# A batched 64x64 matmul: the last 768 matrices of a loaded in tiles of 256, all cast on the way

## The chip, the cores and the metric

The kernel runs on one core of one Trainium2 chip. The core has five engines that run their own instruction streams: TensorE (PE in the profile, with its weight loads as PEld), VectorE (DVE), ScalarE (ACT), GpSimd (POOL) and SyncE (SP). Sixteen DMA engines move data between HBM and the on-chip memory SBUF; SP, ACT and GpSimd each issue transfers on a queue of their own (q1, q10 and q0 in the profile), and all three queues run on the same sixteen engines. Matmul results land in PSUM and are copied out by ACT or DVE. The metric is the device time of the run in microseconds.

## The reference

```python
def setup_inputs():
    return {
        "a": np.random.randn(1024, 64, 64).astype(np.float32),
        "b": np.random.randn(1024, 64, 64).astype(np.float32),
    }

def reference(a: np.ndarray, b: np.ndarray) -> np.ndarray:
    return np.matmul(a, b).astype(np.float32)
```

There are 1024 independent products of two 64x64 matrices. Each operand and the result hold 16.8 MB in float32, so 33.55 MB are read and 16.78 MB written.

## The kernel before, in words

The work goes in 16 steps, t = 0 to 15, of 64 matrices each. One step reads 1 MB of b and writes 1 MB of the result; a is loaded for two steps at a time, in tiles s = 0 to 7 of 128 matrices (2 MB of float32). All instructions stand in an order written out by hand (the block from line 210), and each engine runs its own in that order, so an instruction that waits holds up everything behind it on the same engine.

For one step the chain is this. `load_a` brings a tile of a: three quarters (h = 0 to 2) are transfers that GpSimd issues and that turn float32 into bf16 on the way (line 73), the fourth quarter comes as float32 on SP's queue (line 77). A partition reads 16 rows of a matrix in one run: 4 KB of float32. `regroup` (DVE, lines 108 and 111) copies the four quarters into one bf16 tile, `a_bf`, casting the fourth. `transpose(s, j)` lets TensorE transpose pairs of bf16 values as one 32-bit element (line 120, eight transposes for each j), and ACT copies the results from PSUM to `at_sb` (line 123, four copies for a tile). `spread(t)` (DVE, four copies at line 133) places one step's columns of `at_sb` on the diagonal blocks of one of two tiles `at_bd`. `cast(t)` (DVE, line 144) turns b's tile into bf16. `multiply(t)` runs 64 matmuls of 128x128 by 128x64 (line 189) into two PSUM tiles, one for each half step, and evacuates them to `o_sb` (line 177): eight copies on ACT in an even step; in an odd step six on ACT and two on DVE. `store(t)` sends `o_sb` out, one step later, on GpSimd's queue (line 166; the last two steps go on SP and ACT).

b's tiles come on SP for even t and on ACT for odd t (line 96), three steps ahead: `load_b(t + 3)` is issued once `cast(t)` has freed the buffer. The tiles have 3 buffers for a, 3 for b, 2 for `at_sb`, and 8 for `o_sb`, of which the first two hold the first tile of a before the results need them.

Around one even step t = 2s the order is: `spread(t+1)`, `cast(t+1)`, the second half of the transposes of tile s+1, `multiply(t)`, `regroup(s+2)`; in the odd step after it `spread`, `cast`, `multiply`, and the first half of the transposes of tile s+2. So the transposes that stand ahead of a `multiply` on TensorE work on a tile that was regrouped two steps earlier:

```python
            if half == 0 and 0 < s < n_s - 1:
                transpose(s + 1, 1)
            multiply(t)
```

Of the kernel before, what the change touches and what calls it, by code (L numbers as in the profile page):

```python
# [8 lines left out]
fp32 = mybir.dt.float32  # L9
bf16 = mybir.dt.bfloat16  # L10
# [3 lines left out]
def kernel(  # L14
# [14 lines left out]
    nc = tc.nc  # L29
    B, M, K = a.shape  # L30
    _, _, N = b.shape
    assert (M, K, N) == (64, 64, 64) and B % 128 == 0

    n_t, n_s = B // 64, B // 128
    A_AHEAD = 3
    B_AHEAD = 3
    N_BD = 2
    HOLD = 2

    a_v = a.rearrange("(s g h) (mp v) k -> s h g mp (v k)", h=4, g=32, v=16)  # L40
    b_v = b.rearrange("(t g h) (kp u) n -> t (h kp) g (u n)", h=4, g=16, u=2)
    o_v = out.rearrange("(t gh x) (mo w) n -> t (x mo) gh (w n)", gh=8, x=8, w=4)

    consts = ctx.enter_context(tc.tile_pool(name="consts", bufs=1))
    a_pool = ctx.enter_context(tc.tile_pool(name="a_pool", bufs=A_AHEAD))
    b_pool = ctx.enter_context(tc.tile_pool(name="b_pool", bufs=B_AHEAD))
    work = ctx.enter_context(tc.tile_pool(name="work", bufs=2))
    o_pool = ctx.enter_context(tc.tile_pool(name="o_pool", bufs=8))
    t_psum = ctx.enter_context(
        tc.tile_pool(name="t_psum", bufs=4, space=bass.MemoryType.PSUM)  # L50
    )
# [7 lines left out]
    identity = consts.tile([128, 128], fp32)  # L59
    warm = consts.tile([128, 2], fp32)  # L60
    a_tiles, b_tiles, abf_tiles, at_tiles, bbf_tiles = {}, {}, {}, {}, {}
# [4 lines left out]
            return nc.gpsimd  # L66
        return nc.scalar if t == n_t - 1 and lo % 4 == 0 else nc.sync

    def load_a(s):

        a_sb = a_pool.tile([128, 3, 16, 64], bf16, name="a_sb")
        for h in range(3):
            nc.gpsimd.dma_start(  # L73
                out=a_sb[:, h, :, :].rearrange("p v k -> p (v k)"), in_=a_v[s, h]
            )
        a_raw = a_pool.tile([128, 16, 64], fp32, name="a_raw")
        nc.sync.dma_start(out=a_raw[:].rearrange("p v k -> p (v k)"), in_=a_v[s, 3])
        a_tiles[s] = a_sb, a_raw

    def load_first_a():  # L80

        raw = [
            o_pool.tile([128, 8, 2, 2, 64], fp32, name="o_sb")[:].rearrange(
                "p gh j wl n -> p (gh j wl n)"
            )
            for _ in range(2)
        ]
        parts = [raw[h % 2][:, 1024 * (h // 2) : 1024 * (h // 2) + 1024] for h in range(4)]
        for h in range(4):
            (nc.scalar if h % 2 else nc.sync).dma_start(out=parts[h], in_=a_v[0, h])  # L90
        a_tiles[0] = parts

    def load_b(t):
        b_sb = b_pool.tile([128, 16, 128], fp32, name="b_sb")
        queue = nc.scalar if t % 2 else nc.sync
        queue.dma_start(out=b_sb[:], in_=b_v[t])  # L96
        b_tiles[t] = b_sb

    def regroup(s):
        a_sb = a_tiles.pop(s)  # L100
        a_bf = work.tile([128, 16, 4, 64], bf16, name="a_bf")
        if s == 0:
            for h in range(4):
                copy = nc.scalar.copy if h % 2 else nc.vector.tensor_copy
                copy(a_bf[:, :, h, :], a_sb[h].rearrange("p (v k) -> p v k", v=16))  # L105
        else:
            cast_sb, raw = a_sb
            nc.vector.tensor_copy(  # L108
                a_bf[:, :, 0:3, :], cast_sb[:].rearrange("p h v k -> p v h k")
            )  # L110
            nc.vector.tensor_copy(a_bf[:, :, 3, :], raw[:])  # L111
        abf_tiles[s] = a_bf
        at_tiles[s] = work.tile([128, 2, 32, 2, 4, 4], fp32, name="at_sb")

    def transpose(s, j):
        a_cols = abf_tiles[s][:].rearrange("p v h k -> p v (h k)").bitcast(fp32)
        for wl in range(2):
            at_ps = t_psum.tile([128, 4, 128], fp32, name="at_ps")
            for vo in range(4):
                nc.tensor.transpose(  # L120
                    at_ps[:, vo, :], a_cols[:, 4 * vo + 2 * j + wl, :], identity[:]
                )
            nc.scalar.copy(  # L123
                at_tiles[s][:, j, :, wl, :, :],
                at_ps[:].rearrange("p vo (g mp) -> p g mp vo", mp=4),
            )

    def spread(t):
        half = slice(16 * (t % 2), 16 * (t % 2) + 16)
        bd = bd_tiles[t % N_BD]  # L130
        for h in range(4):
            rows = slice(32 * h, 32 * h + 32)
            nc.vector.tensor_copy(  # L133
                bd[rows, :, :, :, h, :].rearrange("p j g wl mo -> p j (g wl) mo"),
                at_tiles[t // 2][rows, :, half, :, :, :].rearrange(
                    "p j g wl mp vo -> p j (g wl) (mp vo)"
                ),
            )

    def cast(t):  # L140
        b_bf = work.tile([128, 16, 128], bf16, name="b_bf")
        b_sb = b_tiles.pop(t)
        if t < n_t - 1:
            (nc.vector.tensor_copy if t else nc.scalar.copy)(b_bf[:], b_sb[:])  # L144
        else:
            for gq in range(4):
                rows = slice(4 * gq, 4 * gq + 4)
                if gq % 2:
                    nc.vector.tensor_copy(b_bf[:, rows, :], b_sb[:, rows, :])
                else:  # L150
                    nc.scalar.copy(b_bf[:, rows, :], b_sb[:, rows, :])  # L151
        bbf_tiles[t] = b_bf

    def store(t):
        for piece in held.pop(t):
            piece()

    def multiply(t):
# [6 lines left out]
        def put(lo, n):  # L165
            store_queue(t, lo).dma_start(  # L166
                out=o_v[t, :, lo : lo + n, :],
                in_=o_sb[:, lo : lo + n].rearrange("p gh j wl n -> p (gh j wl n)"),
            )
# [36 lines left out]
        else:  # L206
            whole = t < n_t - 2
            held[t] = [lambda q=q: put(q, 8 if whole else 4) for q in ([0] if whole else [0, 4])]

    with tc.manual_schedule():  # L210
        load_first_a()

        nc.vector.memset(warm[:, 0:1], 0.0)
        nc.scalar.copy(warm[:, 1:2], warm[:, 0:1])  # L214
        load_b(0)
        load_b(1)
        nc.vector.memset(bd_tiles[0][:], 0.0)  # L217
        make_identity(nc, identity)
        nc.gpsimd.memset(bd_tiles[1][:, 0], 0.0)
        load_a(1)  # L220
        load_b(2)
        nc.gpsimd.memset(bd_tiles[1][:, 1], 0.0)
        load_a(2)
        regroup(0)
        transpose(0, 0)
        transpose(0, 1)
        spread(0)
        cast(0)
        for t in range(n_t):
            s, half = t // 2, t % 2  # L230
            if t + 1 < n_t:
                spread(t + 1)
                cast(t + 1)
            if t + B_AHEAD < n_t:
                load_b(t + B_AHEAD)
            if half == 0 and 0 < s < n_s - 1 - A_AHEAD:
                load_a(s + 1 + A_AHEAD)
            if half == 0 and 0 < s < n_s - 1:
                transpose(s + 1, 1)
            multiply(t)  # L240
            if t == 0:
                regroup(1)
                load_a(A_AHEAD)
                load_a(A_AHEAD + 1)
                transpose(1, 0)
                transpose(1, 1)
            elif t == 1:
                regroup(2)
            elif half == 0 and s + 2 < n_s:
                regroup(s + 2)  # L250
            if half == 1 and s + 2 < n_s:
                transpose(s + 2, 0)
            if t >= HOLD - 1:
                store(t - HOLD + 1)
        for t in range(n_t - HOLD + 1, n_t):
            store(t)
# [30 lines left out]
```

## Time and profile before

| what | value |
|---|---|
| time, median of 3 runs | 134.86 us (134.75 to 134.9) |
| span of the profiled execution | 133.1 us |
| time of the runs less that span | 1.76 us (134.86 less 133.1) |
| DVE busy | 94.5 us (71%) |
| ACT busy | 87.8 us (66%) |
| PE busy | 65.7 us (49%) |
| DMA, HBM bytes over the span | 378 GB/s |
| mean granted TensorE clock | 0.806 |

The time of the profiled execution by itself is not listed; its span is set beside the runs' median, and the 1.76 us between them are taken as what lies around a span. The page gives busy time by engine, then the span in 40 slices of 3.33 us, in tenths: a row of 9s is an engine that hardly rests. The DMA row is the mean over the sixteen DMA engines. In the DMA table a casting transfer is listed by the bytes it writes (256 KB for each load of line 73), which is half of what it reads.

### The profile page before, as it was taken

The numbers are of one execution on the slowest core, as the hardware profiler recorded it, in microseconds if no ns is written. First come the engines' busy times: TensorE is split into PE (matmuls) and PEld (weight loads), VectorE is DVE, ScalarE is ACT, GpSimd is POOL, SyncE is SP. The second block draws the span as 40 slices with busy tenths as digits, with TensorE's granted clock in tenths as the row PEclk, the third lists the DMA queues.
The fourth block names the chain that finished last, engine by engine and source line by source line (L and its number), as shares of the span: only waits on it lengthen the run. The fifth ranks groups of instructions, "written<-read, shape, count | busy, mean of one in ns | idle before, by whom it ended". The sixth has DMA issues, their size and how long they took to land.

```text
span 133.1 us, 2837 instructions
## 1 busy us (share of the span) xinstructions
PE 65.7 (49%) x1152; PEld 62.7 (47%) x1152; DVE 94.5 (71%) x120; ACT 87.8 (66%) x161; POOL 33.7 (25%) x43
## 2 busy tenths in 40 slices
PE   0005504990068386059519672986199361776000
PEld 0005304980068275058509562975199360766000
DVE  5930299208999719598999699969999994978100
ACT  3134505899128999919899759696969987099600
POOL 8981000420082072143144022203020410210000
PEclk9999999999559999968996875579756985556855
DMA  3999999999999999999999999999999999999991
GB/s 75 367 332 311 307 312 279 278 307 326 328 307 402 316 322 334 393 385 401 318 282 365 402 397 356 308 307 387 395 396 387 393 396 391 402 403 402 380 339 41
DMA packets 19021, 45.01 MB, mean 338 GB/s; under 512 B 1088, under 2 KB 3136, under 8 KB 19008
## 3 DMA queue, kind: packets, MB, share of 16 engines
q0 software_dynamic: 6832, 20.19, 50.2%
q1 hardware_dynamic: 7120, 14.68, 30.5%
q10 hardware_dynamic: 5056, 9.96, 19.8%
q8 instruction: 9, 0.15, 0.4%
q14 instruction: 4, 0.03, 0.1%
HBM read 33.55 MB, written 16.78 MB: 378 GB/s over the span
## 4 chain that ended last, share of the span: by engine, by line
DMA 54%; DVE 18%; ACT 13%; issue 4%; PE 3%; SPq 1%; DVEq 0%; ACTq 0%
DMA b_sb<-in_b_dram 54%; ACT o_sb L177 9%; DVE at_bd L133 9%; DVE b_bf L144 4%; DVE o_sb L177 3%; PE at_ps L120 2%; ACT at_sb L123 2%; ACT b_bf L144 1%; PE o_ps L189 1%; DVE a_bf L108 1%; SPq L90 1%; DVE a_bf L111 1%; ACT b_bf L151 1%; SPq L96 0%; DVEq L133 0%
## 5 line engine op out<-in xcount | busy, mean ns | idle before, releaser
L177 ACT COPY o_sb<-o_ps 64x512 f32<-64x512 f32 x106 | 61.6, 581 | 9.5 <-PE o_ps L189 8.2
L189 PEld LDWEIGHTS <-at_bd 128*128 128x128 bf16 x1024 | 42.5, 113 | 39.7 <-DVE b_bf L144 26.8
L189 PE MATMUL o_ps<-b_bf,at_bd 128*128 128x64 bf16 x960 | 41.2, 213 | 36.0 <-DVE b_bf L144 25.1
L133 DVE COPY at_bd<-at_sb 32x1024 f32<-32x1024 f32 x64 | 46.6, 728 | 13.6 <-ACT at_sb L123 11.8
L120 PE MATMUL at_ps<-identity,a_bf 128*128 128x128 f32 x128 | 22.5, 350 | 19.3 <-ACT a_bf L105 11.4
L166 POOL DMA_DIRECT2D out_dram<-o_sb x14 | 16.3, 1166 | 55.4 <-ACT at_sb L123 23.0
L120 PEld LDWEIGHTS at_ps<-identity,a_bf 128*128 128x128 f32 x128 | 20.7, 190 | 19.4 <-issue 19.4
L144 DVE CAST b_bf<-b_sb 128x2048 bf16<-128x2048 f32 x14 | 17.5, 1249 | 10.0 <-DMA b_sb<-in_b_dram 9.8
L123 ACT COPY at_sb<-at_ps 128x512 f32<-128x512 f32 x32 | 17.4, 590 | 9.9 <-PE at_ps L120 7.6
L73 POOL DMA_DIRECT2D a_sb<-in_a_dram x21 | 13.3, 650 | 27.3 <-DVE a_bf L108 20.4
L177 DVE COPY o_sb<-o_ps 64x512 f32<-64x512 f32 x14 | 9.7, 690 | 0.3
L108 DVE COPY a_bf<-a_sb 128x3072 bf16<-128x3072 bf16 x7 | 7.4, 1059 | 0.0
L105 ACT CAST a_bf<-o_sb 128x1024 bf16<-128x1024 f32 x2 | 2.1, 1044 | 5.3 <-DMA o_sb<-in_a_dram 5.3
L111 DVE CAST a_bf<-a_raw 128x1024 bf16<-128x1024 f32 x7 | 4.8, 683 | 0.0
L144 ACT CAST b_bf<-b_sb 128x2048 bf16<-128x2048 f32 x1 | 1.9, 1897 | 4.1 <-DMA b_sb<-in_b_dram 4.1
L177 DVE COPY o_sb<-at_ps 64x256 f32<-64x256 f32 x8 | 3.4, 422 | 1.3 <-PE at_ps L189 1.2
L105 DVE CAST a_bf<-o_sb 128x1024 bf16<-128x1024 f32 x2 | 2.6, 1296 | 2.4 <-DMA o_sb<-in_a_dram 2.3
L189 PE MATMUL at_ps<-b_bf,at_bd 128*128 128x64 bf16 x64 | 3.6, 242 | 1.0 <-DVE at_bd L133 1.0
L217 DVE MEMSET at_bd<- 128x4096 f32 x1 | 3.5, 3472 | 0.8 <-issue 0.8
L151 ACT CAST b_bf<-b_sb 128x512 bf16<-128x512 f32 x2 | 1.1, 615 | 4.3 <-DMA b_sb<-in_b_dram 4.3
L177 ACT COPY o_sb<-at_ps 64x256 f32<-64x256 f32 x8 | 2.9, 367 | 0.1
L214 ACT ACT_TABLE_LOAD x1 | 1.3, 1283 | 2.3 <-issue 2.3
(12 smaller groups left out, 6.1 us busy)
## 6 DMA issues: line engine op xcount, KB each, us to landing
out_dram<-o_sb POOLq DMA_DIRECT2D x14, 1024.0 KB, 22.3
a_sb<-in_a_dram POOLq DMA_DIRECT2D x21, 256.0 KB, 16.4
a_raw<-in_a_dram SPq DMA_DIRECT2D x7, 512.0 KB, 19.1
o_sb<-in_a_dram SPq DMA_DIRECT2D x2, 512.0 KB, 6.2
o_sb<-in_a_dram ACTq DMA_DIRECT2D x2, 512.0 KB, 7.3
out_dram<-o_sb SPq DMA_DIRECT2D x2, 512.0 KB, 7.4
out_dram<-o_sb SPq DMA_DIRECT2D x2, 256.0 KB, 7.7
out_dram<-o_sb ACTq DMA_DIRECT2D x2, 256.0 KB, 5.9
```

Of the source, the lines that this page charges most:

```text
L73: nc.gpsimd.dma_start(out=a_sb[:, h, :, :].rearrange("p v k -> p (v k)"), in_=a_v[s, h])
L105: copy(a_bf[:, :, h, :], a_sb[h].rearrange("p (v k) -> p v k", v=16))
L108: nc.vector.tensor_copy(a_bf[:, :, 0:3, :], cast_sb[:].rearrange("p h v k -> p v h k"))
L111: nc.vector.tensor_copy(a_bf[:, :, 3, :], raw[:])
L120: nc.tensor.transpose(at_ps[:, vo, :], a_cols[:, 4 * vo + 2 * j + wl, :], identity[:])
L123: nc.scalar.copy(at_tiles[s][:, j, :, wl, :, :], at_ps[:].rearrange("p vo (g mp) -> p g mp vo", mp=4),)
L133: nc.vector.tensor_copy(bd[rows, :, :, :, h, :].rearrange("p j g wl mo -> p j (g wl) mo"), at_tiles[t // 2][rows, :, half, :, :, :].rearrange(
L144: (nc.vector.tensor_copy if t else nc.scalar.copy)(b_bf[:], b_sb[:])
L166: store_queue(t, lo).dma_start(out=o_v[t, :, lo : lo + n, :], in_=o_sb[:, lo : lo + n].rearrange("p gh j wl n -> p (gh j wl n)"),)
L177: copies[2 * par + wl](dst, src)
L189: nc.tensor.matmul(o_ps[:, gl, g % 2, j, :], at_bd[:, j, g, :, u], b_bf[:, g, 64 * u : 64 * u + 64], start=(u == 0), stop=(u == 1),)
L217: nc.vector.memset(bd_tiles[0][:], 0.0)
```

## The change

a is cut differently. The first two tiles keep 128 matrices; the other 768 come as three tiles of 256 (s = 2, 3, 4), so that one partition's run is 32 rows, 8 KB. All four quarters of every tile but the first are now casting loads of GpSimd; SP carries none of a after the first tile. `load_a` takes a list of quarters, so that tiles 3 and 4 can be issued in two halves at different steps. `regroup(s, quad)` copies 16 of the 32 rows of each run, one half tile, in one DVE instruction over 4096 elements, and `transpose(s, quad, part)` now does four transposes and one ACT copy. The tile `at_sb` of a large tile is twice as long and serves four steps. a has 2 buffers instead of 3 and `o_sb` 7 instead of 8.

The places of these steps are listed in a table: `at(t, 0, ...)` puts a step ahead of `multiply(t)`, `at(t, 1, ...)` behind it.

```diff
-    a_v = a.rearrange("(s g h) (mp v) k -> s h g mp (v k)", h=4, g=32, v=16)
+    sizes = [128, 128] + [256] * ((B - 256) // 256)
...
+    def a_rows(s, h):
+        part = a[bases[s] : bases[s] + sizes[s]]
+        part = part.rearrange("(g h) (mp v) k -> h g mp (v k)", h=4, v=sizes[s] // 8)
+        return part[h]
...
-    a_pool = ctx.enter_context(tc.tile_pool(name="a_pool", bufs=A_AHEAD))
+    a_pool = ctx.enter_context(tc.tile_pool(name="a_pool", bufs=2))
...
-    o_pool = ctx.enter_context(tc.tile_pool(name="o_pool", bufs=8))
+    o_pool = ctx.enter_context(tc.tile_pool(name="o_pool", bufs=7))
...
-    def load_a(s):
-
-        a_sb = a_pool.tile([128, 3, 16, 64], bf16, name="a_sb")
-        for h in range(3):
+    def load_a(s, hs=range(4)):
+
+        v = sizes[s] // 8
+        if s not in a_tiles:
+            a_tiles[s] = a_pool.tile([128, 4, v, 64], bf16, name="a_sb")
+        for h in hs:
             nc.gpsimd.dma_start(
-                out=a_sb[:, h, :, :].rearrange("p v k -> p (v k)"), in_=a_v[s, h]
-            )
-        a_raw = a_pool.tile([128, 16, 64], fp32, name="a_raw")
-        nc.sync.dma_start(out=a_raw[:].rearrange("p v k -> p (v k)"), in_=a_v[s, 3])
-        a_tiles[s] = a_sb, a_raw
+                out=a_tiles[s][:, h, :, :].rearrange("p v k -> p (v k)"), in_=a_rows(s, h)
+            )
...
-            cast_sb, raw = a_sb
             nc.vector.tensor_copy(
-                a_bf[:, :, 0:3, :], cast_sb[:].rearrange("p h v k -> p v h k")
-            )
-            nc.vector.tensor_copy(a_bf[:, :, 3, :], raw[:])
+                a_bf[:],
+                a_tiles[s][:, :, 16 * quad : 16 * quad + 16, :].rearrange("p h v k -> p v h k"),
+            )
...
+    def transpose(s, quad, part):
+        j, wl = part // 2, part % 2
+        g, mp = sizes[s] // 4, 512 // sizes[s]
+        if quad == 0 and part == 0:
+            at_tiles[s] = work.tile([128, 2, g, 2, mp, sizes[s] // 32], fp32, name="at_sb")
...
+        at(0, 1, regroup, 1, 0)
+        at(0, 1, load_a, 3, (0, 1))
+        for part in range(4):
+            at(0, 1, transpose, 1, 0, part)
+        at(0, 1, regroup, 2, 0)
+        at(1, 1, regroup, 2, 1)
+        at(1, 1, load_a, 3, (2, 3))
+        at(4, 0, load_a, 4, (0, 1))
+        at(5, 0, load_a, 4, (2, 3))
+        for part in range(4):
+            at(1, part > 1, transpose, 2, 0, part)
+            at(2, part > 1, transpose, 2, 1, part)
+            at(4 + part // 2, part % 2, transpose, 3, 0, part)
+            at(6, part > 1, transpose, 3, 1, part)
+            at(8 + part // 2, part % 2, transpose, 4, 0, part)
+            at(10, part > 1, transpose, 4, 1, part)
+        at(3, 1, regroup, 3, 0)
+        at(5, 1, regroup, 3, 1)
+        at(7, 1, regroup, 4, 0)
+        at(9, 1, regroup, 4, 1)
...
-            if half == 0 and 0 < s < n_s - 1 - A_AHEAD:
-                load_a(s + 1 + A_AHEAD)
-            if half == 0 and 0 < s < n_s - 1:
-                transpose(s + 1, 1)
+            for what, args in steps[t][0]:
+                what(*args)
             multiply(t)
...
+            for what, args in steps[t][1]:
+                what(*args)
```

More of the change, by code (lines that the diff above doesn't have):

```diff
@@ L32 @@
     assert (M, K, N) == (64, 64, 64) and B % 128 == 0
-    n_t, n_s = B // 64, B // 128
-    A_AHEAD = 3
+    n_t = B // 64
     B_AHEAD = 3
@@ L38 @@
     HOLD = 2
-    a_v = a.rearrange("(s g h) (mp v) k -> s h g mp (v k)", h=4, g=32, v=16)
+    sizes = [128, 128] + [256] * ((B - 256) // 256)
+    bases = [sum(sizes[:s]) for s in range(len(sizes))]
+    assert sum(sizes) == B
+    a_of = [s for s, n in enumerate(sizes) for _ in range(n // 64)]
+    first_t = [base // 64 for base in bases]
+    def a_rows(s, h):
+        part = a[bases[s] : bases[s] + sizes[s]]
+        part = part.rearrange("(g h) (mp v) k -> h g mp (v k)", h=4, v=sizes[s] // 8)
+        return part[h]
     b_v = b.rearrange("(t g h) (kp u) n -> t (h kp) g (u n)", h=4, g=16, u=2)
@@ L89, in load_first_a @@
         for h in range(4):
-            (nc.scalar if h % 2 else nc.sync).dma_start(out=parts[h], in_=a_v[0, h])
+            (nc.scalar if h % 2 else nc.sync).dma_start(out=parts[h], in_=a_rows(0, h))
         a_tiles[0] = parts
@@ L97, in load_b, with regroup @@
         b_tiles[t] = b_sb
-    def regroup(s):
-        a_sb = a_tiles.pop(s)
+    def regroup(s, quad):
         a_bf = work.tile([128, 16, 4, 64], bf16, name="a_bf")
@@ L104, in regroup @@
                 copy = nc.scalar.copy if h % 2 else nc.vector.tensor_copy
-                copy(a_bf[:, :, h, :], a_sb[h].rearrange("p (v k) -> p v k", v=16))
+                copy(a_bf[:, :, h, :], a_tiles[0][h].rearrange("p (v k) -> p v k", v=16))
         else:
-            cast_sb, raw = a_sb
             nc.vector.tensor_copy(
-                a_bf[:, :, 0:3, :], cast_sb[:].rearrange("p h v k -> p v h k")
-            )
[L111 to L121, printed above, removed]
-                )
-            nc.scalar.copy(
-                at_tiles[s][:, j, :, wl, :, :],
-                at_ps[:].rearrange("p vo (g mp) -> p g mp vo", mp=4),
-            )
+                a_bf[:],
+                a_tiles[s][:, :, 16 * quad : 16 * quad + 16, :].rearrange("p h v k -> p v h k"),
+            )
+        abf_tiles[s, quad] = a_bf
+    def transpose(s, quad, part):
[3 more added lines that the diff above has]
+            at_tiles[s] = work.tile([128, 2, g, 2, mp, sizes[s] // 32], fp32, name="at_sb")
+        a_cols = abf_tiles[s, quad][:].rearrange("p v h k -> p v (h k)").bitcast(fp32)
+        at_ps = t_psum.tile([128, 4, 128], fp32, name="at_ps")
+        for vo in range(4):
+            nc.tensor.transpose(at_ps[:, vo, :], a_cols[:, 4 * vo + part, :], identity[:])
+        nc.scalar.copy(
+            at_tiles[s][:, j, :, wl, :, 4 * quad : 4 * quad + 4],
+            at_ps[:].rearrange("p vo (g mp) -> p g mp vo", mp=mp),
+        )
     def spread(t):
-        half = slice(16 * (t % 2), 16 * (t % 2) + 16)
+        s = a_of[t]
+        lo = 16 * (t - first_t[s])
         bd = bd_tiles[t % N_BD]
@@ L134, in spread @@
                 bd[rows, :, :, :, h, :].rearrange("p j g wl mo -> p j (g wl) mo"),
-                at_tiles[t // 2][rows, :, half, :, :, :].rearrange(
+                at_tiles[s][rows, :, lo : lo + 16, :, :, :].rearrange(
                     "p j g wl mp vo -> p j (g wl) (mp vo)"
@@ L208, in multiply, with at @@
             held[t] = [lambda q=q: put(q, 8 if whole else 4) for q in ([0] if whole else [0, 4])]
+    steps = {t: ([], []) for t in range(n_t)}
+    def at(t, behind, what, *args):
+        steps[t][behind].append((what, args))
     with tc.manual_schedule():
@@ L223 @@
         load_a(2)
-        regroup(0)
-        transpose(0, 0)
-        transpose(0, 1)
+        regroup(0, 0)
+        for part in range(4):
+            transpose(0, 0, part)
         spread(0)
         cast(0)
+        at(0, 1, regroup, 1, 0)
[7 more added lines that the diff above has]
+        at(5, 0, load_a, 4, (2, 3))
+        for part in range(4):
+            at(1, part > 1, transpose, 2, 0, part)
[8 more added lines that the diff above has]
+        at(9, 1, regroup, 4, 1)
         for t in range(n_t):
-            s, half = t // 2, t % 2
             if t + 1 < n_t:
@@ L235 @@
                 load_b(t + B_AHEAD)
-            if half == 0 and 0 < s < n_s - 1 - A_AHEAD:
-                load_a(s + 1 + A_AHEAD)
-            if half == 0 and 0 < s < n_s - 1:
-                transpose(s + 1, 1)
+            for what, args in steps[t][0]:
+                what(*args)
             multiply(t)
[L241 to L252, printed above, removed]
+            for what, args in steps[t][1]:
+                what(*args)
             if t >= HOLD - 1:
```

## The prediction

> **What bounds the kernel now.** I read the page's slices first, then the DMA queues in a stretch where all three run, then the DVE, PE and ACT timelines of one pair of steps.
>
> ```profile
> PE 65.7 (49%) x1152; PEld 62.7 (47%) x1152; DVE 94.5 (71%) x120; ACT 87.8 (66%) x161; POOL 33.7 (25%) x43
> DVE  5930299208999719598999699969999994978100
> DMA  3999999999999999999999999999999999999991
> HBM read 33.55 MB, written 16.78 MB: 378 GB/s over the span
> L177 ACT COPY o_sb<-o_ps 64x512 f32<-64x512 f32 x106 | 61.6, 581 | 9.5 <-PE o_ps L189 8.2
> L133 DVE COPY at_bd<-at_sb 32x1024 f32<-32x1024 f32 x64 | 46.6, 728 | 13.6 <-ACT at_sb L123 11.8
> L144 DVE CAST b_bf<-b_sb 128x2048 bf16<-128x2048 f32 x14 | 17.5, 1249 | 10.0 <-DMA b_sb<-in_b_dram 9.8
> L123 ACT COPY at_sb<-at_ps 128x512 f32<-128x512 f32 x32 | 17.4, 590 | 9.9 <-PE at_ps L120 7.6
> L108 DVE COPY a_bf<-a_sb 128x3072 bf16<-128x3072 bf16 x7 | 7.4, 1059 | 0.0
> L111 DVE CAST a_bf<-a_raw 128x1024 bf16<-128x1024 f32 x7 | 4.8, 683 | 0.0
> ```
>
> The DMA engines never rest from the second slice to the second last, so DMA sets the time: 50.33 MB of HBM traffic in about 128 us. DVE is close behind: mostly 9s from slice 18 on. Its own work there is about 5.9 us a step (94.5 / 16), against the 6.4 us a step that the kernel keeps; the difference is mainly the 9.8 us for which casts wait for b. A change that adds more than this to the compute chain hands the bound to it.
>
> Packets in the stretch 10 to 18 us, where q0 carries 4 KB casting reads and q1 and q10 carry b:
>
> ```profile
> q0 software_dynamic: 417, 0.76, 49.9%
> q1 hardware_dynamic: 416, 0.85, 30.6%
> q10 hardware_dynamic: 417, 0.85, 27.4%
> ```
>
> Equal counts: the engines take one packet from each queue in turn, and bytes go by packet size. By the bytes read (0.76 MB written by casts are 1.52 MB read) this is 3.22 MB in 8 us, 402 GB/s; b's packets hold 2048 bytes (0.85 MB / 416).
>
> One pair of steps on DVE, PE and ACT:
>
> ```profile
> 63.02 1.23 DVE L144 CAST b_bf<-b_sb 128x2048 bf16<-128x2048 f32 x1 [0.57 <-DMA b_sb<-in_b_dram]
> 64.28 1.39 DVE L177 COPY o_sb<-o_ps 64x512 f32<-64x512 f32 x2
> 65.70 2.83 DVE L133 COPY at_bd<-at_sb 32x1024 f32<-32x1024 f32 x4
> 68.57 1.23 DVE L144 CAST b_bf<-b_sb 128x2048 bf16<-128x2048 f32 x1
> 71.55 3.19 DVE L133 COPY at_bd<-at_sb 32x1024 f32<-32x1024 f32 x4
> 64.31 1.11 PE L189 MATMUL o_ps<-b_bf,at_bd 128*128 128x64 bf16 x32 [1.24 <-DVE b_bf L144]
> 66.05 4.74 ACT L177 COPY o_sb<-o_ps 64x512 f32<-64x512 f32 x8
> ```
>
> multiply(6) starts at 64.31, right behind cast(6): the transposes ahead of it work on a tile that was regrouped long before. ACT has emptied step 6 by 70.8, before DVE asks for spread(8) at 71.55. DVE and ACT run side by side, and spread never waits after the start.
>
> **The change part by part.** Sums are in the profiled span (133.1 us); the runs' median of 134.86 lies 1.76 us above it.
>
> *Bytes and packets.* HBM bytes are the same, and a cast load costs the engines by what it reads: a 4 KB read takes 172 ns with the cast (q0) and 176 ns without (q1's 4 KB packets), means over the trace's packets. So casting the fourth quarter saves DMA 896 packets x 4 ns / 16 = 0.2 us. The 8 KB packet isn't in the trace for a queue of data. From 1 KB (46 ns), 2 KB (88) and 4 KB (172) the next doubling is 334 to 344; 1536 such packets in 16 engines gain 0 to 1.0 us of DMA time. I take 0.5, nearer to nothing since 2 KB to 4 KB shows 4 ns. Fewer loads (16 against 21 on POOL, seven off SP) gain no time: queues are filled ahead, with DMA at 9 throughout.
> The Trainium skill ("DMA: Bandwidth & Descriptors", Anatomy of one DMA) gives every such DMA a fixed 2.0 us; twelve fewer would be 24 us by that sum, but here these overlap, and the sum stays as it is.
>
> *Regroup.* Seven pairs of 1059 + 683 ns go (12.2 us). Seven copies of 4096 elements come: by the early L108 copies (956 ns for 3072) 1.27 us each, 8.9. DVE gains 3.3 us over the run, 0.2 a step. ACT's copies and the transposes keep count and size.
>
> *Tile 2 lands late (new wait).* regroup(2,0) stands on DVE behind regroup(1,0), ahead of spread(2), cast(2) and step 1's evacuation, and needs all of tile 2: 4.19 MB, which q0 starts when tile 1's four loads are through. Before, q0's first four loads were through at 19.2 us. From there three queues share 402 GB/s as 8192 : 2048 : 2048, so q0 gets 268 and the tile lands at 19.2 + 15.6 = 34.8. If q0 moved 4 KB packets it would get half, 201: 40.1. If ACT's queue is empty for a time, q0 gets 80%: 13.0, so 32.2. I take 34.8. b2 has as many packets and lands with it. DVE idled from 24.1 to 30.42 before (at_sb); now it goes on to 34.8.
> From 34.8: regroup 1.3, spread(2) 2.9, cast 1.25, evacuation 1.4, regroup(2,1) 1.3: 43.0. On PE multiply(1) and multiply(2) are now behind transposes of tile 2, so ACT evacuates step 2 only at 46.0 to 50.8, then two at_sb copies to 51.9. spread(4) needs them (an at_sb serves four steps and is complete only with its second half), while DVE is done with cast(3) at 47.1: 4.9 us of new stall. cast(4) ends at 56.1, against 50.6 before, where it had waited for b.
>
> *Each further large tile (new wait).* DVE runs cast(6), evacuation(5), regroup(3,1), and only then may PE do two of that half's transposes, multiply(6) and the other two. Call the end of regroup R. Transposes 1.0, first half of multiply 1.1 and its latency 0.2: ACT evacuates at R + 2.4, eight copies 4.74, two at_sb copies 1.1: spread(8) starts at R + 8.3, or R + 9.8 with PE at half clock (64 matmuls took 3.6 there, 2.03 at full); 8.9 by the mean clock of 0.81. DVE has only spread(7) and cast(7) meanwhile, 4.3. So 4.6 us of stall, for tiles 3 and 4.
> R = 56.1 + evacuation 1.4 + regroup 1.3 + spread(5), cast(5), spread(6), cast(6) 8.2 + 1.4 + 1.3 = 69.7. spread(8) starts at 78.6 (71.55 before). From there spreads of 3.0: spread(8), cast, evacuation, regroup, then two spreads and casts, evacuation, regroup: 18.1, R' = 96.7. Again 8.9: spread(12) at 105.6. Four spreads (12.0), three casts (3.8), two evacuations (2.8): spread(15) ends at 124.2; before it ended at 118.3.
>
> *The end.* Before, the last store was issued at 125.5, 7.2 us behind spread(15), because ACT had waited for b15 until 116.5. Now b15, freed by cast(12) at 109.9, needs some 10 us and lands before it is wanted, so ACT evacuates step 14 from 121.4 to 126.1 and step 15 to 129.4. The 2 MB of these two steps' stores take 5.4 us at 390 GB/s: from 126.1 + 1.5 to 133.0; before, packets ended at 131.4, and the span 1.7 later. Sum: 133.0 + 1.7 = 134.7 of span. The new bound is 1.6 us beyond the old; with 1.76 around it, about 136.4.
>
> *Buffers and queues.* POOL issues four more 8 KB loads behind step 0's order and the stores follow; the a4 halves stand between stores 2, 3 and 4. With q0 drained at the shares above, tile 4 lands near 83, just before regroup(4,0) at 84.2: cost 0, up to 3 if q0 is slower. Seven o_sb buffers: step 7 reuses step 0's, stored by 54, and needs it after 74: 0. SP loses seven a_raw issues: b's even tiles start earlier, but after 50 us casts wait for DVE, not for b: 0.
>
> The same page (Queues, rings and completion order) says each engine drains a packet of about 9 to 17 descriptors before it turns; with 512-byte descriptors of b against 8 KB runs q0 would have 89%, tile 2 would land at 30.9, and the sum would be 3.9 us less; the counts 417, 416, 417 speak for the packets as the profile lists them.
>
> **The rivals.** (1) *Tile 2 later.* The 8 KB runs go as 4 KB packets: tile 2 at 40.1, all behind it 5.3 later: 141.7; half of that 139. For: nothing in the data queues has moved 8 KB. Against: packets of a's loads are whole runs today. (2) *DMA stays the bound, ending faster.* The stalls are shorter than I draw them, because DMA is 1.6 us behind my chain only; then the span is 133.1 less 0.5 to 1.2, and the time 133.6 to 134.4. It decides when tile 2 lands before 33 or spread(8) waits under 3.8 us. (3) *No difference:* DMA stays the bound and 8 KB packets gain nothing, 134.86.
>
> **How the numbers follow.** Forecast case 0.52, with its own range 135.2 to 138.5 (half clock at both waits +1.8, tile 2 at 32.2 or q0 slower by 2); rival 1 0.17; rival 2 0.24; rival 3 0.07. 0.2% (0.27 us) is what a measurement of this kernel can tell from no change. Faster 0.24, same 0.07, slower 0.69. The range 133.9 to 140.5 leaves out the far ends of rivals 1 and 2.
>
> **What would show it.** regroup(2,0) at L114 waiting for a_sb until about 35 us; spread at L140 waiting for ACT's at_sb near 47, 74 and 101, 4 to 5 us each; few waits of casts for b; DMA slices below 9 after 100 us; q0 with 8 KB reads at 330 to 345 ns. The prediction is wrong if DVE shows no such waits, or if tile 2 lands before 33.

## The result, and the profile after

The changed kernel takes 150.81 us (median of 4 runs, 150.21 to 150.86) against 134.81 us before: 1.118 times as long, 95% interval 1.116 to 1.120. The direction was right and the size was not: 16 us were lost where 1.6 were forecast, and the time lies far outside the range of 133.9 to 140.5.

From the page of the changed kernel (busy time by engine, the slices, HBM bytes, the groups that answer to those shown before):

```profile
PE 68.2 (46%) x1152; PEld 64.6 (43%) x1152; DVE 90.4 (61%) x113; ACT 88.3 (59%) x161; POOL 29.9 (20%) x38
DVE  5520892008559329998197089993791499989800
DMA  3999999999999999999999999989996859784991
HBM read 33.55 MB, written 16.78 MB: 338 GB/s over the span
...
L184 ACT COPY o_sb<-o_ps 64x512 f32<-64x512 f32 x106 | 61.5, 580 | 12.5 <-PE o_ps L196 10.5
L140 DVE COPY at_bd<-at_sb 32x1024 f32<-32x1024 f32 x64 | 46.6, 728 | 23.5 <-ACT at_sb L129 21.4
...
L151 DVE CAST b_bf<-b_sb 128x2048 bf16<-128x2048 f32 x14 | 17.2, 1227 | 0.4
L184 DVE COPY o_sb<-o_ps 64x512 f32<-64x512 f32 x14 | 9.6, 689 | 11.2 <-ACT o_sb L184 11.0
L114 DVE COPY a_bf<-a_sb 128x4096 bf16<-128x4096 bf16 x7 | 8.6, 1226 | 10.8 <-DMA a_sb<-in_a_dram 10.6
```

Busy time hardly moved: DVE has 4.1 us less work, ACT 0.5 us more. What moved is idle time. Casts no longer wait for b (0.4 us before L151, 10.0 before), and from slice 31 on the DMA row is below 9 in six of seven slices (6, 8, 5, 7, 8 and 4): DMA is no longer the bound there. DVE instead waits three times over: 10.6 us for tile 2 of a, 21.4 us for ACT's `at_sb` (11.8 before), and 11.0 us in front of its own evacuation copies, for ACT's evacuation copies. In the kernel before, all idle time in front of these copies is 0.3 us:

```profile
L177 DVE COPY o_sb<-o_ps 64x512 f32<-64x512 f32 x14 | 9.7, 690 | 0.3
```

Lines of DVE, ACT and PE between 69 and 90 us, around step 6 (start, duration, engine, line and operation; in brackets the idle time before it and what ended it):

```profile
69.25 1.23 DVE L151 CAST b_bf<-b_sb 128x2048 bf16<-128x2048 f32 x1
73.98 1.39 DVE L184 COPY o_sb<-o_ps 64x512 f32<-64x512 f32 x2 [3.50 <-ACT o_sb L184]
75.40 1.23 DVE L114 COPY a_bf<-a_sb 128x4096 bf16<-128x4096 bf16 x1
76.55 3.20 DVE L140 COPY at_bd<-at_sb 32x1024 f32<-32x1024 f32 x4
79.78 1.23 DVE L151 CAST b_bf<-b_sb 128x2048 bf16<-128x2048 f32 x1
86.27 2.83 DVE L140 COPY at_bd<-at_sb 32x1024 f32<-32x1024 f32 x4 [5.26 <-ACT at_sb L129]
```
```profile
72.17 1.78 ACT L184 COPY o_sb<-o_ps 64x512 f32<-64x512 f32 x3
73.97 0.58 ACT L129 COPY at_sb<-at_ps 128x512 f32<-128x512 f32 x1
77.84 0.58 ACT L129 COPY at_sb<-at_ps 128x512 f32<-128x512 f32 x1 [3.28 <-PE at_ps L128]
78.69 0.59 ACT L129 COPY at_sb<-at_ps 128x512 f32<-128x512 f32 x1 [0.27 <-PE at_ps L128]
80.40 4.74 ACT L184 COPY o_sb<-o_ps 64x512 f32<-64x512 f32 x8 [1.12 <-PE o_ps L196]
85.16 1.07 ACT L129 COPY at_sb<-at_ps 128x512 f32<-128x512 f32 x2
```
```profile
69.46 1.09 PE L196 MATMUL o_ps<-b_bf,at_bd 128*128 128x64 bf16 x32 [0.80 <-ACT o_sb L184]
...
76.69 1.97 PE L128 MATMUL at_ps<-identity,a_bf 128*128 128x128 f32 x8 [5.66 <-DVE a_bf L114]
78.45 3.13 PE L196 MATMUL o_ps<-b_bf,at_bd 128*128 128x64 bf16 x64
```

This is a ring of three engines. DVE ends cast(6) at 70.48 and then waits 3.50 us until ACT's last copy of step 5 ends at 73.95. It does not wait for the matmuls of that half step, which end at 70.55, nor for ACT's data: ACT's two copies of the half step write partitions 0 to 63 of `o_sb`, DVE's two write 64 to 127. DVE's copies stand behind ACT's in the program, both write one tile, and the profile shows the one released by the other; no run takes that link away. Only then it may do regroup(3,1), behind which PE waits with the transposes and multiply(6) (5.66 us idle). ACT waits for PE (3.28 us), so its evacuation of step 6 and the last `at_sb` copies end at 86.23, and DVE waits 5.26 us more for the last `at_sb`. Each engine rests while the next one works; the same picture comes again 31 us later (waits of 3.51 us at 105.26 and 5.30 us at 117.59).

The loads did what the queue counts promised. From 26 to 34 us, when q0 carries 8 KB reads:

```profile
q0 software_dynamic: 290, 1.06, 65.1%
q1 hardware_dynamic: 294, 0.57, 20.8%
q10 hardware_dynamic: 295, 0.60, 19.5%
```

Equal counts again, 290, 294 and 295, and q0's packet now reads 8 KB where b's has 2 KB: its share of the engines goes from half to two thirds. Tile 2's first regroup starts at 34.01 us.

### The profile page after: what moved, and what is told of

Same layout as the page of the kernel before. It is cut to its first block, busy times and chain, and to the rows that moved or that the text cites. A ratio compares the mean times of both kernels' runs of the same rounds, so it can differ in the third digit from the quotient of the medians.

```text
span 149.0 us, 2798 instructions
## 1 busy us (share of the span) xinstructions
PE 68.2 (46%) x1152; PEld 64.6 (43%) x1152; DVE 90.4 (61%) x113; ACT 88.3 (59%) x161; POOL 29.9 (20%) x38
## 4 chain that ended last, share of the span: by engine, by line
DVE 26%; DMA 26%; ACT 18%; PE 14%; POOL 6%; issue 3%; ACTq 1%; DVEq 0%; POOLq 0%
DMA a_sb<-in_a_dram 17%; ACT o_sb L184 15%; DVE at_bd L140 11%; DMA out_dram<-o_sb 10%; DVE o_sb L184 8%; PE o_ps L196 7%; PE at_ps L128 6%; DVE a_bf L114 4%; DVE b_bf L151 3%; ACT at_sb L129 3%; POOL a_sb L84 3%; POOL at_bd L234 2%; POOL at_bd L231 1%; PE at_ps L196 1%; ACTq L104 1%
## 5 line engine op out<-in xcount | busy, mean ns | idle before, releaser
L184 ACT COPY o_sb<-o_ps 64x512 f32<-64x512 f32 x106 | 61.5, 580 | 12.5 <-PE o_ps L196 10.5
L140 DVE COPY at_bd<-at_sb 32x1024 f32<-32x1024 f32 x64 | 46.6, 728 | 23.5 <-ACT at_sb L129 21.4
L196 PEld LDWEIGHTS <-at_bd 128*128 128x128 bf16 x1024 | 45.2, 116 | 25.1 <-issue 10.6
L196 PE MATMUL o_ps<-b_bf,at_bd 128*128 128x64 bf16 x960 | 44.5, 220 | 21.3 <-DVE b_bf L151 7.9
L128 PE MATMUL at_ps<-identity,a_bf 128*128 128x128 f32 x128 | 24.9, 359 | 48.1 <-DVE a_bf L114 37.1
L129 ACT COPY at_sb<-at_ps 128x512 f32<-128x512 f32 x32 | 17.9, 589 | 27.1 <-PE at_ps L128 26.9
L173 POOL DMA_DIRECT2D out_dram<-o_sb x14 | 15.4, 1102 | 91.5 <-ACT o_sb L184 44.5
L151 DVE CAST b_bf<-b_sb 128x2048 bf16<-128x2048 f32 x14 | 17.2, 1227 | 0.4
L114 DVE COPY a_bf<-a_sb 128x4096 bf16<-128x4096 bf16 x7 | 8.6, 1226 | 10.8 <-DMA a_sb<-in_a_dram 10.6
L84 POOL DMA_DIRECT2D a_sb<-in_a_dram x16 | 9.9, 668 | 13.7 <-DVE a_bf L114 13.7
L151 ACT CAST b_bf<-b_sb 128x2048 bf16<-128x2048 f32 x1 | 1.9, 1899 | 4.0 <-DMA b_sb<-in_b_dram 4.0
L112 DVE CAST a_bf<-o_sb 128x1024 bf16<-128x1024 f32 x2 | 1.5, 744 | 3.2 <-DMA o_sb<-in_a_dram 3.2
L196 PE MATMUL at_ps<-b_bf,at_bd 128*128 128x64 bf16 x64 | 2.0, 194 | 1.4 <-DVE at_bd L140 1.4
L234 POOL MEMSET at_bd<- 128x2048 f32 x1 | 2.3, 2309 | 0.0
```

The lines of the kernel that those rows point to most:

```text
L84: nc.gpsimd.dma_start(out=a_tiles[s][:, h, :, :].rearrange("p v k -> p (v k)"), in_=a_rows(s, h))
L112: copy(a_bf[:, :, h, :], a_tiles[0][h].rearrange("p (v k) -> p v k", v=16))
L114: nc.vector.tensor_copy(a_bf[:], a_tiles[s][:, :, 16 * quad : 16 * quad + 16, :].rearrange("p h v k -> p v h k"),)
L128: nc.tensor.transpose(at_ps[:, vo, :], a_cols[:, 4 * vo + part, :], identity[:])
L129: nc.scalar.copy(at_tiles[s][:, j, :, wl, :, 4 * quad : 4 * quad + 4], at_ps[:].rearrange("p vo (g mp) -> p g mp vo", mp=mp),)
L140: nc.vector.tensor_copy(bd[rows, :, :, :, h, :].rearrange("p j g wl mo -> p j (g wl) mo"), at_tiles[s][rows, :, lo : lo + 16, :, :, :].rea ...
```

## The experiments

In each run only what the diff shows is changed. The kernel before was run beside each group and gave 134.89 to 135.14 us; ratios below are to those runs.

**Tiles 3 and 4 in the old order.** `at(t, ...)` is moved so that each half is regrouped a step before its transposes stand ahead of a multiply.

```diff
-            at(4 + part // 2, part % 2, transpose, 3, 0, part)
-            at(6, part > 1, transpose, 3, 1, part)
-            at(8 + part // 2, part % 2, transpose, 4, 0, part)
-            at(10, part > 1, transpose, 4, 1, part)
-        at(3, 1, regroup, 3, 0)
-        at(5, 1, regroup, 3, 1)
-        at(7, 1, regroup, 4, 0)
-        at(9, 1, regroup, 4, 1)
+        for s, t0 in ((3, 3), (4, 7)):
+            at(t0, 1, regroup, s, 0)
+            at(t0 + 1, 1, regroup, s, 1)
+            for quad in range(2):
+                for part in range(4):
+                    at(t0 + 1 + quad + part // 2, part < 2, transpose, s, quad, part)
```

> The changed kernel with only the places of tiles 3 and 4 moved: each half is regrouped a step before it is needed, and the transposes stand behind one multiply and ahead of the next, as in the kernel before. Theory (the order of regroup, transposes and multiply makes ACT late, and DVE waits for ACT): both 5.3 us waits of spread for at_sb (at 86 and 117 us) and the 3.5 us waits of DVE's evacuation for ACT after 70 us go; cast(4) ended at 59.1 as against 50.6 before, so from there the old pace gives 82.5 us more, a span of 135 to 141, a time of 137 to 143. Rival (the 8 KB loads starve b or the stores): 148 us or more.

Measured: 139.85 us (2 runs), 11 us less than the changed kernel, inside the expected 137 to 143. DVE's waits by releaser in this run (what waited and for whom; us in total, times, the longest):

```profile
DVE a_bf L114 <- DMA a_sb<-in_a_dram: 11.4, 1, 11.4
DVE at_bd L140 <- ACT at_sb L129: 10.7, 2, 5.5
DVE o_sb L184 <- ACT o_sb L184: 5.7, 3, 3.3
DVE b_bf L151 <- DMA b_sb<-in_b_dram: 3.8, 1, 3.8
```

The two at_sb waits of tiles 3 and 4 are gone (21.4 us are now 10.7, the one at the start and that of tile 2), the evacuation waits halve (two of 1.2 us, after 110 us, are left where I had expected none), and a cast waits for b again. The order of the steps accounts for 11 us; the large loads are still there.

**DVE takes the first two copies.**

```diff
                 if half and t % 2:
-                    copies[2:] = [nc.vector.tensor_copy] * 2
+                    copies[:2] = [nc.vector.tensor_copy] * 2
```

> The changed kernel with only this changed: in an odd step's second half DVE takes the first two of the four evacuation copies and ACT the last two, so that ACT waits for DVE and not DVE for ACT. Theory (DVE's evacuation waits for ACT, with regroup and the next multiply queued behind it): the three waits of 3.4 to 3.5 us go and the time falls by 8 to 11 us to 140 to 143. Rival (only the late at_sb counts, the evacuation's wait is slack that at_sb gives back): within 2 us of 150.8.

Measured: 137.18 us (136.73 and 137.63), 13.6 us less, more than expected. All large tiles and their order are unchanged, and each engine does as many copies of the same size; DVE's now write partitions 0 to 63, and who waits for whom is turned round (ACT waits for DVE, 3.40 us at 56.77 and 3.87 us at 83.42). DVE's evacuation starts as soon as the matmuls allow (it waits 1.7 us for them in all), and spread(8) starts at 77.34 us as against 86.27:

```profile
51.16 2.83 DVE L140 COPY at_bd<-at_sb 32x1024 f32<-32x1024 f32 x4 [3.79 <-ACT at_sb L129]
...
65.29 1.23 DVE L151 CAST b_bf<-b_sb 128x2048 bf16<-128x2048 f32 x1
66.64 1.39 DVE L184 COPY o_sb<-o_ps 64x512 f32<-64x512 f32 x2
67.96 1.21 DVE L114 COPY a_bf<-a_sb 128x4096 bf16<-128x4096 bf16 x1
69.09 3.08 DVE L140 COPY at_bd<-at_sb 32x1024 f32<-32x1024 f32 x4
74.50 1.23 DVE L151 CAST b_bf<-b_sb 128x2048 bf16<-128x2048 f32 x1 [2.33 <-DMA b_sb<-in_b_dram]
77.34 2.83 DVE L140 COPY at_bd<-at_sb 32x1024 f32<-32x1024 f32 x4 [1.61 <-ACT at_sb L129]
...
104.01 2.83 DVE L140 COPY at_bd<-at_sb 32x1024 f32<-32x1024 f32 x4 [3.78 <-ACT at_sb L129]
```
```profile
69.22 1.09 PE L128 MATMUL at_ps<-identity,a_bf 128*128 128x128 f32 x8 [2.14 <-DVE a_bf L114]
70.15 2.03 PE L196 MATMUL o_ps<-b_bf,at_bd 128*128 128x64 bf16 x64
```

The waits for `at_sb` shrink too (21.4 to 14.8 us), for another reason. From the end of a regroup to the spread that waits, this run takes 8.05, 8.17 and 8.18 us where the changed kernel takes 9.70, 9.64 and 9.68, since PE ran faster: around step 6 the eight transposes took 1.09 us instead of 1.97 and the 64 matmuls 2.03 instead of 3.13, at a granted clock of 1.00 (68 to 72 us) against 0.50 (76 to 80 us in the changed kernel). Over the three places that is 4.6 us. Both runs of this kernel have a mean clock of 0.80, against 0.75 to 0.78 in the four of the changed kernel, so the faster PE came with the swap; why is not shown. The wait at 77.34 is as short as 1.61 us only because DVE has spent 2.33 us waiting for b just before; the other two are still 3.8 us. The rival, that at_sb gives the gain back, falls.

**The same change on the kernel before.**

```diff
                 if half and t % 2:
-                    copies[2:] = [nc.vector.tensor_copy] * 2
+                    copies[:2] = [nc.vector.tensor_copy] * 2
```

> The kernel before with the swapped evacuation alone. Theory: before, ACT has ended the step when DVE comes to its two copies, and DMA is the bound, so nothing changes: 134.3 to 135.3. Rival (the wait costs there too): 131 to 134.

Measured: 135.01 us, ratio 1.0001 (0.9985 to 1.0018). No difference: before, ACT is done with the step when DVE comes to it.

**4 KB runs.** The loads of large tiles are cut in two.

```diff
         for h in hs:
-            nc.gpsimd.dma_start(
-                out=a_tiles[s][:, h, :, :].rearrange("p v k -> p (v k)"), in_=a_rows(s, h)
-            )
+            for q in range(v // 16):
+                nc.gpsimd.dma_start(
+                    out=a_tiles[s][:, h, 16 * q : 16 * q + 16, :].rearrange("p v k -> p (v k)"),
+                    in_=a_rows(s, h)[:, :, 1024 * q : 1024 * q + 1024],
+                )
```

> The changed kernel with each load of a large tile cut in two, rows 0 to 15 and 16 to 31 of each run, so that all of a comes in 4 KB runs again, 28 casting loads in all; nothing else. Theory (order of the steps, not the size of the runs): q0's share falls from two thirds to a half, tile 2 lands near 40 and not 34, and since all that follows hangs on it the time is 152 to 157 us. Rival (the 8 KB run itself is what costs): well below 150.8, 138 to 145.

Measured: 153.18 us (2 runs), 2.4 us more than the changed kernel. regroup(2,0) starts at 36.77 us instead of 34.01, 2.8 us later (less than expected; from 20 to 28 us ACT's queue, q10, is nearly empty in both kernels, with 125 packets here against 549 of q0, and 90 against 324 in the changed kernel), and the whole run is later by about as much; the waits for at_sb (20.9 us) and for ACT's evacuation (10.9 us) are what they were. The 8 KB run itself is not what costs; in this order of steps it is a small gain.

**Seven result buffers alone**, on the kernel before.

```diff
-    o_pool = ctx.enter_context(tc.tile_pool(name="o_pool", bufs=8))
+    o_pool = ctx.enter_context(tc.tile_pool(name="o_pool", bufs=7))
```

> The kernel before with seven result buffers instead of eight, nothing else. Theory: the eighth buffer is not needed, 134.4 to 135.3. Rival (stores land late enough for step 7 to wait for step 0's buffer): 136 to 140.

Measured: 135.03 us, ratio 1.0017 (0.9997 to 1.0037): no difference to be seen.

**Tile 2 in another order.**

```diff
-        at(0, 1, regroup, 2, 0)
+        at(1, 1, regroup, 2, 0)
         at(1, 1, regroup, 2, 1)
...
-            at(1, part > 1, transpose, 2, 0, part)
-            at(2, part > 1, transpose, 2, 1, part)
+            at(1, 1, transpose, 2, 0, part)
+            at(2, 0, transpose, 2, 1, part)
```

> The changed kernel with only tile 2's steps moved: both its regroups stand behind step 1's evacuation on DVE, all transposes of its first half behind multiply(1), all of its second half ahead of multiply(2). Theory: spread(4) no longer waits for copies of at_sb behind step 2's evacuation and starts near 45 instead of 55 us; cast(4) then waits for b4 until about 49 as in the kernel before, so some 8 us go, 142 to 145. Rival (tile 2's landing at 34 us is what holds the start, whatever the order): 149 to 151.

Measured: 143.9 us (2 runs), 6.9 us less. spread(4) starts at 44.30 us instead of 55.00, while tile 2 lands no earlier (its slowest load takes 26.5 us from issue to landing, against 24.8): its landing is covered when spread(2), cast(2) and the evacuation of step 1 stand ahead of the regroup that waits for it.

**Repairs together**: the order of tiles 3 and 4 with the swapped copies; all three; and the order of all three tiles without the swap. The edits are those above.

> The moved steps of tiles 3 and 4 and the swapped evacuation together; tile 2 as in the changed kernel. Theory (two waits, of which either repair alone left part): cast(4) ends near 55 as with the swap alone, then at the pace of DMA 82 us less what 8 KB packets save (1536 packets at 322 ns instead of 344, 2 us): span 133 to 135, time 134.5 to 137. Rival (the two repairs save the same microseconds): 137.

> All three repairs: tile 2's steps, those of tiles 3 and 4, and the swapped evacuation. Theory: nothing waits for ACT, DMA is the bound again, with 2 us less of DMA time for a's 8 KB packets: 132.5 to 134.5. Rival (large tiles hold back b by their share of the queues, whatever the order): 135 or more.

> The changed kernel with the steps of all three large tiles moved, and DVE's evacuation as in the changed kernel, last. Theory (the evacuation's wait is long only because the order makes ACT late): with the order repaired DVE finds ACT done, as before, and the time is within 1 us of the run with all three repairs: 135.5 to 137.5. Rival (the evacuation's wait is a cost by itself): 139 or more.

| repaired | time, us |
|---|---|
| nothing | 150.81 |
| tile 2's order | 143.90 |
| tiles 3 and 4's order | 139.85 |
| swapped copies | 137.18 |
| tiles 3 and 4, swapped copies | 136.00 |
| order of all three tiles | 136.83 |
| all three | 136.56 |
| kernel before | 134.89 to 135.14 |

By themselves the repairs gain 6.9, 11.0 and 13.6 us, 31.5 together, where 16 were lost: they are cuts of one ring, and after each of the three combinations DMA is full again up to 118 or 121 us. The order of all three tiles alone, with DVE's copies last, reaches 136.83, and DVE waits for ACT's evacuation there 3.8 us in all, instead of 11.0. So most of that wait comes of an order that makes ACT late, as the theory had it, but not all of it goes: one of 3.36 us is left at 51.84, where ACT runs twelve copies without a break from 43.48 us on. None of the three reached the kernel before; for all three repairs together I had expected 132.5 to 134.5, and that was wrong (ratio 1.011, 1.007 to 1.015); with two it is 1.007 (1.005 to 1.009). The time is the rival's, 135 or more; that its reason holds, large tiles that hold back b, is not shown: casts wait for b 7.3 us in all there, 9.8 us in the kernel before.

Where the last microsecond is, by stretch (us; busy time and instructions of PE, PEld, DVE, ACT and POOL; granted clock, DMA share, GB/s): first the run with two repairs, then the kernel before.

```profile
100.00:120.00 20.00, 11.41 (x235) 11.03 (x236) 17.10 (x23) 15.78 (x29) 3.12 (x3) 0.72 1.03 386
120.00:128.00 8.00, 3.75 (x89) 3.62 (x86) 5.25 (x12) 7.54 (x15) 1.05 (x1) 0.71 0.84 294
```
```profile
100.00:120.00 20.00, 12.30 (x237) 11.86 (x237) 16.67 (x22) 14.92 (x28) 3.62 (x3) 0.67 1.03 396
120.00:128.00 8.00, 1.97 (x37) 1.81 (x34) 3.38 (x8) 5.31 (x13) 0.00 (x0) 0.71 1.04 387
```

Up to 120 us both keep DMA full. Then the kernel before still has stores to move while it computes its last two steps (share 1.04), and the repaired one runs dry (0.84). ACT gets b's last tile at 120.26 us instead of 116.54, and the stores of the last two steps come later; that this is the cause was tried next.

**b's last two tiles early.** In the buffer that tile 3 of a has left, two steps earlier than before.

```diff
+    late = []
...
+        if t < n_t - 2:
+            b_sb = b_pool.tile([128, 16, 128], fp32, name="b_sb")[:]
+        else:
+            if t == n_t - 2:
+                late.append(a_pool.tile([128, 2, 16, 128], fp32, name="a_sb"))
+            b_sb = late[0][:, t % 2, :, :]
...
-            if t + B_AHEAD < n_t:
+            if t + B_AHEAD < n_t - 2:
                 load_b(t + B_AHEAD)
+            if t in (9, 10):
+                load_b(t + 5)
```

> The two repairs (tiles 3 and 4, swapped evacuation), and b's last two tiles loaded into the buffer that tile 3 of a has left, issued in steps 9 and 10 instead of 11 and 12. Theory (with the waits gone what is left of the loss is the end: b15 lands at 120.6 us instead of 116.0, and the DMA engines idle a fifth of 120 to 128 us): b15 lands before 112, the stores fill the end, 1 to 2 us go, 134.0 to 135.2. Rival (the rest of the loss is the share that large packets take from b all along): 135.6 to 136.5.

> All three repairs and the early load of b's last two tiles. Theory: as the run beside it, DMA the bound to the end, 133.5 to 135.2. Rival: 135.6 or more.

Measured: 137.92 and 138.90 us, both slower than without the edit. ACT now issues b15 right behind b13, and that second issue holds ACT. With all three repairs:

```profile
96.69 0.69 ACTq L110 DMA_DIRECT2D b_sb<-in_b_dram  x1
...
97.85 4.39 ACTq L110 DMA_DIRECT2D a_sb<-in_b_dram  x1
98.17 0.59 ACT L135 COPY at_sb<-at_ps 128x512 f32<-128x512 f32 x1
102.28 1.07 ACT L135 COPY at_sb<-at_ps 128x512 f32<-128x512 f32 x2 [3.53 <-issue]
```

The issue takes 4.39 us instead of 0.69, and at_sb and the evacuations behind it are 3.53 us late. So the edit brought a new wait, and says nothing on its question. Both loads were therefore put on SP:

```diff
-        queue = nc.scalar if t % 2 else nc.sync
+        queue = nc.scalar if t % 2 and t < n_t - 2 else nc.sync
```

> As the early load of b's last two tiles with two repairs, but both are issued on SP, so that ACT's second load in a row (4.13 us, with at_sb and the evacuations behind it) is not there. Theory (the end is what is left): b15 lands before 118, 134.0 to 135.5. Rival (the end is not what is left): 136 or more.

Measured: 136.49 us, ratio 1.012 (1.010 to 1.015). ACT is free again, but b15 now queues behind b14 on SP and ACT gets it at 120.92 us, no earlier than without the edit, and the DMA share from 120 to 128 us is 0.73. By the expectation's letter the rival holds, but its premise, an earlier b15, did not come about. What would be gained by an earlier b15 stays open.

## Why the prediction was wrong, step by step

*Bytes and packets.* 8 KB casting packets were put at 334 to 344 ns. They took 322 ns (median from 20 to 44 us), so the DMA gain was 1536 x 22 / 16 = 2.1 us instead of 0.5. It did not count, since DMA was no longer the bound. The 24 us that the prediction sets beside the sum, 2.0 us for each of twelve loads, take in seven loads of SP, while the section that it cites from the Trainium skill ("DMA: Bandwidth & Descriptors", Anatomy of one DMA) is on DMAs that GpSimd issues: five fewer, 10 us by that figure. Neither is seen here: the run with 4 KB runs has twelve loads more on GpSimd than the changed kernel and lost 2.4 us.

*Regroup.* 1.27 us each forecast, 1.23 measured.

*Tile 2 lands late.* 34.8 forecast, 34.01 measured: the sharing by packet counts held. ACT's queue was nearly empty from 20 to 28 us, which the prediction weighed (32.2, if it were so for a time); 34.01 lies between. The new stall of 4.9 us before spread(4) was 5.33, but spread(4) started at 55.00 instead of 52.0.

*Each further large tile.* The wait for at_sb was forecast at 4.6 us a tile and measured at 5.26 and 5.30; the next spread was to start 8.9 us after the regroup and started 9.6 us after (76.63 to 86.27). The two ends of that estimate both came: 9.8 us at half PE clock (9.6 here, at a granted clock of 0.50 from 76 to 80 us) and 8.3 at full clock (8.2 with the copies swapped, at 1.00 from 68 to 72 us). The wait was right in place and mechanism; taking the mean clock of 0.81 for this stretch made it a little short.

*The rule weighed there.* The Trainium skill ("DMA: Bandwidth & Descriptors", Queues, rings and completion order) has each engine drain a packet of some 9 to 17 descriptors before it turns, which by the prediction's estimate would have landed tile 2 at 30.9 us; the measured 34.01 us and the counts of 290, 294 and 295 speak for one run of q0 to one 2 KB packet of b, and decide.

*The step that failed* is the evacuation of odd steps, which the sum prices at 1.4 us each time, with no wait. DVE's two copies wait for ACT's last copies of the same half step. In the kernel before that wait never shows (0.3 us in all), so the sum has none, although its own term for each large tile makes ACT late. It measured 3.41, 3.50, 3.51 and 0.58 us, 11.0 us together (1.8 more are the longer at_sb waits, less 0.8 for tile 2's earlier landing; 0.8 is left over). spread(15) ended at 136.98 us instead of 124.2, 12.8 us later. The rest of the 14.3 us by which the span exceeds the sum lies behind spread(15): 12.0 us to the end instead of 10.5. With only this wait turned round, the changed kernel takes 137.18 us, beside the 136.4 forecast without it. That the two lie so close is in part chance: spread(15) ends at 122.19 us there, 2.0 us ahead of the forecast, and 13.5 us instead of 10.5 follow it.

*Buffers and queues.* Seven buffers cost nothing, as forecast; regroup(4,0) did not wait for tile 4; casts did not wait for b.

*The rivals.* Tile 2 did not land later. DMA did not stay the bound, and the packets' faster rate could not show. The repaired kernels, where DMA is the bound again, came out 0.9 to 1.9 us above the kernel before and not below it. The forecast had one wait of the ring, spread's for `at_sb`; neither it nor a rival had the other, and so nothing reached beyond 141.7.

The waits listed as signs came: regroup(2,0)'s until 34.01 us, and spread three times, beginning at 49.7, 81.0 and 112.3 us where 47, 74 and 101 were forecast, each later by about what the evacuation's waits had added up to there. The sign for q0, 330 to 345 ns, did not come (322).

## What to carry to other kernels

A wait that costs nothing in a trace may be met early rather than absent: when a change makes the engine that meets it later, price the wait anew, at every place where the two engines touch, and look for a ring (here DVE to PE to ACT and back), because then the waits add up, as they did here, instead of hiding one another. Where two engines share the copies of one result, try to let the engine that the next step waits for go first; that alone gave back 13.6 of the 16 us here (of which some 4.6 go with a PE that ran faster), and did nothing in the kernel before, where DVE did not have to wait. And regroup a tile a full step before the matmul that its transposes stand in front of: for two of the three large tiles that gave back 11.0 us.

## What the runs showed of the hardware that was not expected

A casting read of 8 KB took 322 ns where two of 4 KB took 344 (172 each): the step from 4 to 8 KB adds 150 ns, that from 2 to 4 KB about 84 (from 88 to 172, the shorter ones uncast). With 8 KB packets the three queues still took turns packet by packet (290, 294 and 295 in 8 us).

A second load issued by ACT 1.2 us behind the first, both of 1 MB, kept ACT for 4.39 us instead of 0.69, and the copies behind it 3.53 us. Why it was held (the first load's packets may still have been queued) was not tried.
